# A two-layer diffusion trunk step on one core: four gate columns ahead of the feed-forward pairs, the residual affine on VectorE, two modulation vectors moved

## The chip, the core and the metric

One core of a Trainium2 chip. Its engines run unsynchronized instruction queues: TensorE (PE, matmuls and transposes, with its weight loads listed as PEld), VectorE (DVE), ScalarE (ACT), GpSimd (POOL) and SyncE (SP), which here only issues DMAs. The metric is the device time of one execution in microseconds (us); lower is better.

## What is computed

One inference step of a trunk of two post-norm layers over 512 latent tokens and 128 prompt tokens of width 1024. Each layer mixes the tokens (attention, a delta-rule scan and an HGRN scan), projects, normalizes, and runs a gated feed-forward block. Cut to what the change touches:

```python
def trunk_layer(x, mod, ...):
    shift_m, scale_m, gate_m, shift_f, scale_f, gate_f = jnp.split(mod.astype(x.dtype), 6, axis=-1)
    z = (x * (1 + scale_m) + shift_m) @ w_in
    o, k_c, v_c, s_d, s_h = token_mixers(z, ...)
    x = layer_norm(ALPHA * x + gate_m * (o @ w_out), ln_g[0], ln_b[0])
    gt, up = jnp.split((x * (1 + scale_f) + shift_f) @ w_ffn_in, 2, axis=-1)
    x = layer_norm(ALPHA * x + gate_f * ((jax.nn.silu(gt) * up) @ w_ffn_out), ln_g[1], ln_b[1])
    return x, k_c, v_c, s_d, s_h
# per layer l: mod_p = silu(c_ctx) @ w_mod[l] + b_mod[l], mod_s = silu(c) @ w_mod[l] + b_mod[l]
```

The matrices are float32: w_in 1024 x 3856, w_out 1024 x 1024, w_ffn_in 1024 x 5632 (gate columns, then up columns), w_ffn_out 2816 x 1024, w_mod 1024 x 6144.

## The kernel before

Tokens are five tiles of 128 (four latent, one prompt). A float32 product is made of three matmuls on a high and a low part of both factors: the high part of a weight is a cast on ACT, the low part a subtraction on DVE, both into an `hl` tile (four buffers); the weight itself first lands in a `raw` tile of 512 KB (three buffers, loaded from SP's queue). The code lists the work in program order; a planner orders each engine's instructions by its own estimate of what is ready, and `behind()` keeps the instructions under it after those in `AFTER`, engine by engine.

**Output projection and entry.** `pss` holds five PSUM tiles for columns 0 to 511; the loop takes one weight unit (`rowunit`, two of eight row blocks) after another over all five token tiles, and then `residual` runs for the five tiles: multiply by the gate, `r = ALPHA * x + ...`, statistics, all DVE. Columns 512 to 1023 go tile by tile with the four units of `us1`, and behind each tile `ln_next` normalizes and modulates it and `ffn_T` transposes it into `xT` (transposes named pta). `ffn_sums`, called at tiles 3 and 4, builds the sums and differences of token halves (`fS`, `fA`, `SX`) that the feed-forward product needs: per call eight DVE operations, two on POOL (named fa) and four casts on ACT. `ln_rest` then gives `r` its normalization and affine (one ACT, two POOL operations per tile, the POOL ones `r<-r,lg` and `r<-r,lb`); `r` is needed when part 0 of the output products adds to it.

**Pairs.** The input product of the block runs as one level of a seven-product scheme (Strassen-Winograd) over 22 column blocks f. Column f has a gate half and an up half, each 1024 x 128. `pair_a(f)` takes two of the seven products (pfa, 24 matmuls) with the gate columns `gts[f]`; `pair_b(f)` the other five (pfc, pfb, pfd, 60 matmuls) with sums of gate and up weights: two preparations on POOL (`t<-raw`, `raw<-raw`), two on DVE, three `in_two` (cast and subtraction). `gate_unit(f)` loads both halves and converts the gate half. Pairs stand in the order a0, a1, b0, b1, a2, b2, a3, and so on. After each part of `FF_PARTS` (four pairs in the first) come the output products pfo, 120 matmuls of 512 columns for four pairs; part 0 adds to `r` on DVE, later parts on POOL. The gate rows of the block (modulation vector 5) are loaded into the tiles `lg` and `lb_` once these are free.

**Modulation.** Vectors 3, 4, 2 and 5 of a layer's six are made in `mods()` during its own mixer, turn by turn with attention and HGRN (`run`, `TURNS`): eight loads of w_mod into `raw` and 32 small matmuls (psm) each. Vectors 0 and 1 of layer 1 are made by `modulation_wide` between the pairs of layer 0: loads from POOL's queue, multiply-adds on DVE (`mw`), 32 matmuls in all.

Of the kernel before, what the change touches and what calls it, by code (L numbers as in the profile page):

```python
# [10 lines left out]
F32 = mybir.dt.float32  # L11
# [26 lines left out]
C_AQ, C_AK, C_AV, C_BQKV, C_BG, C_CQ, C_CF, C_CI = 0, 512, 1024, 1536, 2304, 2576, 2832, 3344  # L38
NB = 272
FF_PARTS = ((0, 4), (4, 8), (8, 12), (12, 16), (16, 18), (18, 22))  # L40

# [66 lines left out]
def tile_trunk(  # L108
# [64 lines left out]
    def tt(eng, out, a, b, op):  # L173
        return eng.tensor_tensor(out, a, b, op)  # L174
# [68 lines left out]

    AFFINE = [[((G, G),), ((G, G),)], ((V, V), (G, G),)]

# [236 lines left out]

    def modulation_wide(l, vecs, pool):


        for i in vecs:
            dst = modrow[l][:, i * D:(i + 1) * D].rearrange("j (g n) -> j g n", g=4)
            for j in range(2):
                S.dma_start(bm[QR[j]], b_mod[l][i * D:(i + 1) * D].rearrange("(g n) -> g n", g=4))
            ms = cp.tile([P, 256], F32, tag="ms", name=f"ms{l}_{i}")  # L490
            for hf in range(2):
                w8 = pool.tile([P, 2, 1024], F32, tag="hb", bufs=1, name=f"mw{l}_{i}_{hf}")
                acc, raw2 = (w8[:, x].rearrange("p (j n) -> p j n", j=2) for x in range(2))
                for k in range(KT):
                    raw = raw2[:, k % 2]
                    G.dma_start(raw, w_mod[l][k * P:(k + 1) * P, i * D + 512 * hf:i * D + 512 * hf + 512])
                    for j in range(2):
                        ck = cm[:, k, j:j + 1]
                        if k == 0:
                            A.activation(acc[:, j], raw, AF.Copy, scale=ck)  # L500
                        else:
                            V.scalar_tensor_tensor(acc[:, j], raw, ck, acc[:, j], ALU.mult, ALU.add)
                    if k % 2:
                        yield
                ps = psS("m", f"psm{l}_{i}_{hf}")
                hs = slice(64 * hf, 64 * hf + 64)
                for g in range(2):
                    for j in range(2):
                        mm(ps[64 * hf + 32 * g:64 * hf + 32 * g + 32, :256], onesj[:, j],
                           acc[:, j, g * 256:(g + 1) * 256], start=(j == 0), stop=(j == 1))  # L510
                tt(V, ms[hs], ps[hs, :256], bm[hs], ALU.add)
            for j in range(2):
                S.dma_start(dst[j], ms[QR[j]])

    def rowload(pool, src, tag, t=None):
# [59 lines left out]


    def ln_rest(r, mv, rs, g, b, dst):
        eng = AFFINE[0][CUR[0]] if dst is None else AFFINE[1]
        V.scalar_tensor_tensor(rs[:, :, 1], mv[:, :, 0], -1.0, rs[:, :, 0], ALU.mult, ALU.mult)
        for tau in range(NT):  # L580
            A.activation(r[tau], r[tau], AF.Identity, scale=rs[:, tau, 0:1], bias=rs[:, tau, 1:2])
            em, ea = eng[tau % len(eng)]
            tt(em, r[tau], r[tau], g, ALU.mult)
            tt(ea, r[tau], r[tau], b, ALU.add)
            if dst is not None:
                S.dma_start(dst[tau * P:(tau + 1) * P, :], r[tau])

# [783 lines left out]
    for l in range(DEPTH):  # L1371
# [41 lines left out]
        def mods():  # L1413
            yield from modulation(l, (3, 4, 2, 5))
            yield
            affine(l, 4, 3, (l, 0), praw, "raw", 3)
            yield

        held = {}
# [135 lines left out]
        pss = [psS("n", f"pop{l}_0_{tau}") for tau in range(NT)]  # L1555
        for n_, i in enumerate((2, 3, 0, 1)):
            u = rowunit(w_out[l], 2 * i, 2, 0, 512)
            for tau in range(NT):
                gemm_N(pss[tau], 512, xT, tau, [(u, [2 * i, 2 * i + 1])], first=(n_ == 0), last=(n_ == 3))
        us1 = [(rowunit(w_out[l], 2 * i, 2, 512, 512), [2 * i, 2 * i + 1]) for i in (2, 3, 0, 1)]  # L1560
        for tau in range(NT):
            residual(pss[tau], gm[tau >= LT][:, :512], r[tau], r[tau], 0, st[tau])

        def load_pair(f):
            g_, u_ = (raw_unit(Wi[:, c0 + f * P:c0 + f * P + P].rearrange("(k p) n -> p k n", p=P), KT, P)[0]
                      for c0 in (0, DFF))
            return g_, u_

# [11 lines left out]
        def gate_unit(f):  # L1580
            raws[f] = load_pair(f)
            gts[f] = in_two(raws[f][0], 1024, hl_tile())

        gate_unit(0)
        for tau in range(NT):
# [18 lines left out]

        def mods_wide():
            yield from modulation_wide(l + 1, range(2), fp)
            affine(l + 1, 1, 0, (l, 1), praw, "raw", 3)

        wide = mods_wide() if l + 1 < DEPTH else iter(())


# [14 lines left out]
        def pair_a(f):  # L1626
            if f not in gts:
                gate_unit(f)
            gt_ = gts.pop(f)
            a_ = psS("g", f"pfa{l}_{f}")  # L1630
            prod(a_, gt_, 0, "11")
            s1 = fp.tile([P, HT], F32, tag="s1", bufs=2, name=f"s1_{l}_{f}")
            A.copy(s1, a_[:, :HT])  # L1633
            prod(a_, gt_, 4, "12", start=False)
            sg = fp.tile([P, NTOK], F32, tag="sg", bufs=2, name=f"sg{l}_{f}")
# [44 lines left out]

        pair_a(0)
        pair_a(1)
        for part, (f0, f1) in enumerate(FF_PARTS):
            nk = f1 - f0
            last = part == len(FF_PARTS) - 1
            for f in range(f0, f1):
                pair_b(f, f - f0)
                if 1 <= f < NFF - 1:
                    pair_a(f + 1)
                for _ in range(2):  # L1690
                    next(wide, 0)
            if part == 0:
                gf = [rowload(None, modvec(l, 5, j), None, t_) for j, t_ in enumerate((lg, lb_))]
            if last:
                for _ in wide:
                    pass
# [90 lines left out]
```

## Time and profile before

| what | value |
|---|---|
| median of three runs | 2152.37 us (2149.19 to 2155.8) |
| the profiled execution | 2161.62 us |
| its span, first to last instruction | 2159.5 us |
| mean granted clock of PE, as a share of full | 0.934 |
| busy: PE, DVE, POOL, ACT | 1926.4, 1494.9, 963.1, 809.4 us |

The span holds the start (to 41 us), layer 0's projections and mixer (to 543), its output projection and entry (to 662), its feed-forward block (to 1110), and the same for layer 1 (mixer to about 1593, pair 0 at 1717, end 2160). Stage times below are microseconds from the span's start. A wait in square brackets is idle time of an engine just before the instruction, with what ended it.

### The profile page before, as it was taken

The numbers are of one execution on the slowest core, as the hardware profiler recorded it, in microseconds if no ns is written. First come the engines' busy times: TensorE is split into PE (matmuls) and PEld (weight loads), VectorE is DVE, ScalarE is ACT, GpSimd is POOL, SyncE is SP. The second block draws the span as 40 slices with busy tenths as digits, with TensorE's granted clock in tenths as the row PEclk, the third lists the DMA queues.
The fourth block names the chain that finished last, engine by engine and source line by source line (L and its number), as shares of the span: only waits on it lengthen the run. The fifth ranks groups of instructions, "written<-read, shape, count | busy, mean of one in ns | idle before, by whom it ended". The sixth has DMA issues, their size and how long they took to land. (4 is left out here: it accounts for less than half of the span.)

```text
span 2159.5 us, 37748 instructions
## 1 busy us (share of the span) xinstructions
PE 1926.4 (89%) x14818; PEld 1698.0 (79%) x14818; DVE 1494.9 (69%) x2556; ACT 809.4 (37%) x1582; POOL 963.1 (45%) x1040
## 2 busy tenths in 40 slices
PE   7999997778946999999989999978899399999996
PEld 5988986557736888998979988865677399899995
DVE  5458525767598897676776794358867978666676
ACT  3532312547242333343325423226742343334331
POOL 0374334755173224324354843358642712432444
PEclk8999997887977999999999999989999699999998
DMA  9323226771503433232244232277631132222222
GB/s 298 105 73 123 89 73 161 218 214 41 185 30 94 150 108 88 80 91 76 86 136 137 84 119 86 82 182 230 201 142 54 47 100 72 85 88 89 78 70 77
DMA packets 235334, 245.15 MB, mean 114 GB/s; under 512 B 19498, under 2 KB 182294, under 8 KB 235158
## 3 DMA queue, kind: packets, MB, share of 16 engines
q1 hardware_dynamic: 210422, 214.69, 32.1%
q10 hardware_dynamic: 22176, 19.67, 3.5%
q0 software_dynamic: 2560, 8.39, 1.2%
q8 instruction: 117, 1.92, 0.4%
q14 instruction: 59, 0.48, 0.1%
HBM read 214.52 MB, written 28.18 MB: 112 GB/s over the span
## 5 line engine op out<-in xcount | busy, mean ns | idle before, releaser
L174 DVE TENSOR_TENSOR hl<-raw,hl 128x1024 fp32r<-128x1024 f32 (+1 forms) x210 | 281.1, 1342 | 92.6 <-ACT hl L271 77.3
L171 PE MATMUL pfo<-hl,ha 128*128 128x512 f32 x1320 | 313.4, 395 | 1.1 <-DVE ft L174 0.6
L171 PEld LDWEIGHTS pfo<-hl,ha 128*128 128x128 f32 x1320 | 246.0, 188 | 60.8 <-DVE ft L174 1.3
L174 POOL TENSOR_TENSOR r<-r,ft 128x512 f32<-128x512 f32 x96 | 143.8, 1519 | 250.1 <-DVE ft L174 249.5
L171 PE MATMUL pfc<-sx,hl 128*128 128x320 f32 x1056 | 176.0, 315 | 58.8 <-ACT hl L1571 54.1
L171 PEld LDWEIGHTS pfc<-sx,hl 128*128 128x128 f32 x1056 | 163.1, 192 | 63.7 <-ACT hl L1571 56.3
L171 PE MATMUL pfa<-xT,hl 128*128 128x320 f32 x1056 | 181.7, 321 | 20.5 <-ACT s L1633 10.9
L171 PEld LDWEIGHTS pfa<-xT,hl 128*128 128x128 f32 x1056 | 167.1, 198 | 24.8 <-ACT s L1633 12.2
L174 POOL TENSOR_TENSOR t<-raw 128x512 f32<-128x512 f32 x44 | 64.4, 1463 | 265.2 <-DMA raw<-in_w_ffn_in_dram 119.7
L271 ACT CAST hl<-raw 128x1024 fp32r<-128x1024 f32 (+2 forms) x122 | 125.4, 1035 | 134.1 <-DMA raw<-in_w_ffn_out_dram 44.5
L1571 ACT CAST hl<-raw 128x1024 fp32r<-128x1024 f32 x88 | 92.3, 1051 | 209.9 <-PE pfo L171 96.9
L171 PE MATMUL paq<-xT,hl 128*128 128x320 f32 x768 | 123.2, 317 | 0.6 <-ACT az L1264 0.6
L171 PEld LDWEIGHTS paq<-xT,hl 128*128 128x128 f32 x768 | 115.7, 190 | 3.4 <-issue 1.2
L171 PE MATMUL pop<-hl,xT 128*128 128x512 f32 x480 | 113.3, 395 | 1.1 <-ACT ae_p L1157 1.1
L174 POOL TENSOR_TENSOR hK<-hK,hT 64x256 f32<-64x256 f32 x120 | 90.3, 753 | 42.7 <-PE ph L171 36.6
L171 PEld LDWEIGHTS pop<-hl,xT 128*128 128x128 f32 x480 | 89.1, 188 | 20.8 <-ACT ae_p L1157 1.2
L174 DVE TENSOR_TENSOR ft<-pfo,lg 128x512 f32<-128x512 f32 x96 | 64.2, 683 | 54.8 <-PE pfo L171 48.1
L174 DVE TENSOR_TENSOR t<-raw,t 128x512 f32<-128x512 f32 x88 | 74.4, 845 | 35.3 <-POOL t L174 35.1
L171 PE MATMUL pbq<-xT,hl 128*128 128x320 f32 x576 | 90.1, 314 | 1.0 <-DVE hl L174 0.4
L171 PE MATMUL pfd<-xT,hl 128*128 128x320 f32 x528 | 87.0, 314 | 4.1 <-DVE ft L174 3.4
L171 PE MATMUL pfb<-sx,hl 128*128 128x320 f32 x528 | 89.4, 314 | 0.0
L171 PEld LDWEIGHTS pbq<-xT,hl 128*128 128x128 f32 x576 | 86.0, 190 | 2.6 <-issue 0.8
(404 smaller groups left out, 4371.3 us busy)
## 6 DMA issues: line engine op xcount, KB each, us to landing
raw<-in_w_ffn_in_dram SPq DMA_DIRECT2D x88, 512.0 KB
raw<-in_w_mod_dram SPq DMA_DIRECT2D x64, 512.0 KB
raw<-in_w_in_dram SPq DMA_DIRECT2D x56, 512.0 KB
raw<-in_w_ffn_out_dram SPq DMA_DIRECT2D x44, 512.0 KB
pc<-in_w_mod_dram SPq DMA_DIRECT2D x8, 1024.0 KB
raw<-in_w_out_dram SPq DMA_DIRECT2D x16, 512.0 KB
mw<-in_w_mod_dram POOLq DMA_DIRECT2D x32, 256.0 KB, 3.1
qksc<-az SPq DMA_DIRECT2D x16, 320.0 KB
```

The lines of the kernel that those rows point to most:

```text
L171: nc.tensor.matmul(out, lhsT, rhs, start=start, stop=stop, **kw)
L174: return eng.tensor_tensor(out, a, b, op)
L271: A.copy(hl[:, 0, :kt * n], raw[:, :kt * n])
L1571: A.copy(tile_[:, 0, :n], raw)
```

## The change

- `gate_unit(f)` loads only the gate half for f below `AHEAD` = 4; `pair_b` loads both halves then. `pair_a(0)` to `pair_a(3)` stand ahead of the first `pair_b`; the intermediate results of columns 2 and 3 lie in a new tile `xtra`.
- `ln_rest` is dropped from the entry. `ln_tile` does the same for one tile with two `scalar_tensor_tensor` operations on DVE, called behind pairs 0, 1, 2 (tiles 0 to 2) and 3 (tiles 3 and 4). `ln_rest` stays for the end of layer 0.
- `modulation_wide` is removed; vectors 0 and 1 of layer 1 are made in layer 0's `mods()`, after the other four.
- The first half of the output projection loads all four units first, runs two of them over all tiles, then the other two tile by tile with `residual` behind each tile.

```diff
+AHEAD = 4
...
-    AFFINE = [[((G, G),), ((G, G),)], ((V, V), (G, G),)]
+    AFFINE = ((V, V), (G, G))
...
-    def modulation_wide(l, vecs, pool):
...
+    def ln_tile(r, mv, rs, g, b, tau):
+        V.scalar_tensor_tensor(r[tau], r[tau], mv[:, tau, 0:1], g, ALU.subtract, ALU.mult)
+        V.scalar_tensor_tensor(r[tau], r[tau], rs[:, tau, 0:1], b, ALU.mult, ALU.add)
...
             affine(l, 4, 3, (l, 0), praw, "raw", 3)
             yield
+            if l + 1 < DEPTH:
+                yield from modulation(l + 1, (0, 1))
+                affine(l + 1, 1, 0, (l, 1), praw, "raw", 3)
+                yield
...
-        for n_, i in enumerate((2, 3, 0, 1)):
-            u = rowunit(w_out[l], 2 * i, 2, 0, 512)
-            for tau in range(NT):
-                gemm_N(pss[tau], 512, xT, tau, [(u, [2 * i, 2 * i + 1])], first=(n_ == 0), last=(n_ == 3))
+        us0 = [(rowunit(w_out[l], 2 * i, 2, 0, 512), [2 * i, 2 * i + 1]) for i in (2, 3, 0, 1)]
+        for tau in range(NT):
+            gemm_N(pss[tau], 512, xT, tau, us0[:2], last=False)
+        for tau in range(NT):
+            gemm_N(pss[tau], 512, xT, tau, us0[2:], first=False)
+            residual(pss[tau], gm[tau >= LT][:, :512], r[tau], r[tau], 0, st[tau])
         us1 = [(rowunit(w_out[l], 2 * i, 2, 512, 512), [2 * i, 2 * i + 1]) for i in (2, 3, 0, 1)]
-        for tau in range(NT):
-            residual(pss[tau], gm[tau >= LT][:, :512], r[tau], r[tau], 0, st[tau])
...
         def gate_unit(f):
-            raws[f] = load_pair(f)
-            gts[f] = in_two(raws[f][0], 1024, hl_tile())
+            g_ = load_col(0, f)
+            if f >= AHEAD:
+                raws[f] = (g_, load_col(DFF, f))
+            gts[f] = in_two(g_, 1024, hl_tile())
...
-        with behind():
-            ln_rest(r, mv, rs, lg, lb_, None)
...
-            g_, u_ = raws.pop(f)
+            g_, u_ = raws.pop(f) if f in raws else (load_col(0, f), load_col(DFF, f))
...
-        pair_a(0)
-        pair_a(1)
+        xtra = fp.tile([P, 2048], F32, tag="hb", bufs=1, name=f"xtra{l}")
+        for f in range(AHEAD):
+            pair_a(f)
...
                 pair_b(f, f - f0)
-                if 1 <= f < NFF - 1:
+                if AHEAD - 1 <= f < NFF - 1:
                     pair_a(f + 1)
-                for _ in range(2):
-                    next(wide, 0)
+                if part == 0:
+                    for tau in range(f, NT if f == f1 - 1 else f + 1):
+                        ln_tile(r, mv, rs, lg, lb_, tau)
```

## Rows read from the trace of the kernel before

**Rows 1.** The page, busy us, share of the span and instructions of each engine.
```profile
PE 1926.4 (89%) x14818; PEld 1698.0 (79%) x14818; DVE 1494.9 (69%) x2556; ACT 809.4 (37%) x1582; POOL 963.1 (45%) x1040
```

**Rows 2.** Stretches: length, busy us of five engines, PE's clock, DMA share, GB/s.
```profile
608.00:662.20 54.20, 14.63 (x66) 12.90 (x65) 51.98 (x37) 20.06 (x27) 41.55 (x23) 0.63 0.11 35
662.20:751.40 89.20, 83.79 (x448) 73.27 (x448) 76.67 (x110) 30.15 (x45) 24.94 (x28) 0.94 0.45 139
751.40:842.20 90.80, 84.85 (x473) 75.83 (x474) 77.40 (x111) 28.63 (x42) 29.38 (x26) 0.94 0.31 94
...
1663.00:1716.60 53.60, 16.67 (x73) 14.13 (x73) 51.35 (x37) 19.38 (x28) 42.23 (x17) 0.66 0.03 10
1716.60:1794.00 77.40, 76.85 (x434) 70.33 (x435) 59.21 (x87) 27.41 (x40) 16.34 (x10) 0.97 0.34 102
1794.00:1871.30 77.30, 77.30 (x458) 71.81 (x458) 52.08 (x76) 27.18 (x41) 25.90 (x17) 1.00 0.27 82
```

**Rows 3.** Timeline of PE, entry of layer 1: start, length, instruction, wait before it.
```profile
1664.76 0.64 PE L171 MATMUL pfa<-xT,hl 128*128 128x320 f32 x1 [0.74 <-ACT xT L1517]
...
1686.44 3.29 PE L171 MATMUL pfa<-xT,hl 128*128 128x320 f32 x12 [3.28 <-ACT s L1633]
1716.58 0.90 PE L171 MATMUL pfc<-sx,hl 128*128 128x320 f32 x2 [26.84 <-ACT hl L1571]
```

**Rows 4.** Groups of DVE, 1663 to 1717: busy us, mean ns | idle before.
```profile
L174 DVE TENSOR_TENSOR fs<-fs,xT 128x512 f32<-128x512 f32 x3 | 8.4, 2803 | 0.0
L174 DVE TENSOR_TENSOR sx<-fs,sx 128x768 fp32r<-128x768 f32 x3 | 6.9, 2299 | 1.0 <-ACT sx L1532 1.0
L174 DVE TENSOR_TENSOR sx<-fs,sx 128x512 fp32r<-128x512 f32 x3 | 6.4, 2120 | 0.0
L174 DVE TENSOR_TENSOR fs<-fs,xT 128x768 f32<-128x768 f32 x3 | 5.0, 1658 | 0.0
L174 DVE TENSOR_TENSOR xT<-fa,xT 128x768 fp32r<-128x768 f32 x1 | 3.1, 3094 | 0.0
```

**Rows 5.** Timeline of DVE, both entries, the two shapes while POOL is idle.
```profile
1676.92 0.95 DVE L174 TENSOR_TENSOR fs<-fs,xT 128x768 f32<-128x768 f32 x1
...
650.96 0.68 DVE L174 TENSOR_TENSOR fs<-xT,fs 128x512 f32<-128x512 f32 x1
```

**Rows 6.** Groups of POOL, 1663 to 1717.
```profile
L174 POOL TENSOR_TENSOR r<-r,lg 128x1024 f32<-128x1024 f32 x5 | 15.3, 3067 | 0.0
L174 POOL TENSOR_TENSOR r<-r,lb 128x1024 f32<-128x1024 f32 x5 | 14.4, 2890 | 0.0
```

**Rows 7.** Stretch of layer 1 from pair 0 to the output products, 1717 to 1769.
```profile
sum 52.00, PE 51.45 PEld 49.85 DVE 39.38 ACT 21.10 POOL 12.50; mean PE 25.72 PEld 24.92 DVE 19.69 ACT 10.55 POOL 6.25
```

**Rows 8.** Groups of DVE, 1663 to 1717: a scalar_tensor_tensor of 128x1024.
```profile
L572 DVE SCALAR_TENSOR_TENSOR xma<-r,mv,sc 128x1024 f32<-128x1024 f32 x1 | 1.3, 1274 | 0.0
```

**Rows 9.** Timeline of POOL, part 0 of layer 1, one pair's preparation.
```profile
1752.25 1.30 POOL L174 TENSOR_TENSOR t<-raw 128x512 f32<-128x512 f32 x1 [9.55 <-DMA raw<-in_w_ffn_in_dram]
```

**Rows 10.** Groups of DVE, 662 to 842 (parts 0 and 1 of layer 0).
```profile
L502 DVE SCALAR_TENSOR_TENSOR mw<-mw,cm 128x512 f32<-128x512 f32 x50 | 39.5, 825 | 5.0 <-DMA mw<-in_w_mod_dram 2.7 <-ACT mw L500 2.3
```

**Rows 11.** Stretch of layer 0's mixer behind its last modulation vector, 480 to 543.
```profile
sum 63.00, PE 51.18 PEld 45.88 DVE 50.31 ACT 42.27 POOL 37.47; mean PE 17.06 PEld 15.29 DVE 16.77 ACT 14.09 POOL 12.49
```

**Rows 12.** Timeline of PE in the mixer: eight modulation matmuls.
```profile
462.42 0.64 PE L171 MATMUL psm<-raw,cm 128*32 128x256 f32 x8
```

**Rows 13.** Waits of PE, 385 to 480: us in total, times, longest.
```profile
PE psm L171 <- DMA raw<-in_w_mod_dram: 8.9, 9, 2.7
```

**Rows 14.** SP's queue: the first and last w_mod loads shown, 29 in all.
```profile
394.80 13.93 SPq L252 DMA_DIRECT2D raw<-in_w_mod_dram  x8
...
463.34 8.06 SPq L252 DMA_DIRECT2D raw<-in_w_mod_dram  x5
```

**Rows 15.** Timeline of PE, output projection of layer 0: its first and its last matmuls.
```profile
543.40 5.86 PE L171 MATMUL pop<-hl,xT 128*128 128x512 f32 x24 [1.06 <-ACT ae_p L1157]
...
560.62 36.65 PE L171 MATMUL pop<-hl,xT 128*128 128x512 f32 x156
```

More of the change, by code (lines that the diff above doesn't have):

```diff
@@ L481, in modulation @@
             yield
-    def modulation_wide(l, vecs, pool):
[L486 to L513, printed above, removed]
     def rowload(pool, src, tag, t=None):
@@ L574, in ln_next @@
         return into(xm, tau, f"pt{name}") if into else to_T(xm, xT, tau, f"pt{name}")
+    def ln_tile(r, mv, rs, g, b, tau):
+        V.scalar_tensor_tensor(r[tau], r[tau], mv[:, tau, 0:1], g, ALU.subtract, ALU.mult)
+        V.scalar_tensor_tensor(r[tau], r[tau], rs[:, tau, 0:1], b, ALU.mult, ALU.add)
     def ln_rest(r, mv, rs, g, b, dst):
-        eng = AFFINE[0][CUR[0]] if dst is None else AFFINE[1]
+        eng = AFFINE
         V.scalar_tensor_tensor(rs[:, :, 1], mv[:, :, 0], -1.0, rs[:, :, 0], ALU.mult, ALU.mult)
@@ L584, in ln_rest @@
             tt(ea, r[tau], r[tau], b, ALU.add)
-            if dst is not None:
-                S.dma_start(dst[tau * P:(tau + 1) * P, :], r[tau])
+            S.dma_start(dst[tau * P:(tau + 1) * P, :], r[tau])
     def ln_last(r, st, mv, rs, g, b, tau, dst):
@@ L1555, in tile_trunk, with load_col @@
         pss = [psS("n", f"pop{l}_0_{tau}") for tau in range(NT)]
-        for n_, i in enumerate((2, 3, 0, 1)):
-            u = rowunit(w_out[l], 2 * i, 2, 0, 512)
-            for tau in range(NT):
-                gemm_N(pss[tau], 512, xT, tau, [(u, [2 * i, 2 * i + 1])], first=(n_ == 0), last=(n_ == 3))
-        us1 = [(rowunit(w_out[l], 2 * i, 2, 512, 512), [2 * i, 2 * i + 1]) for i in (2, 3, 0, 1)]
-        for tau in range(NT):
-            residual(pss[tau], gm[tau >= LT][:, :512], r[tau], r[tau], 0, st[tau])
[L1564 to L1567, printed above, removed]
+        us0 = [(rowunit(w_out[l], 2 * i, 2, 0, 512), [2 * i, 2 * i + 1]) for i in (2, 3, 0, 1)]
[4 more added lines that the diff above has]
+            residual(pss[tau], gm[tau >= LT][:, :512], r[tau], r[tau], 0, st[tau])
+        us1 = [(rowunit(w_out[l], 2 * i, 2, 512, 512), [2 * i, 2 * i + 1]) for i in (2, 3, 0, 1)]
+        def load_col(c0, f):
+            return raw_unit(Wi[:, c0 + f * P:c0 + f * P + P].rearrange("(k p) n -> p k n", p=P), KT, P)[0]
         def in_two(raw, n, tile_):
@@ L1603, in tile_trunk @@
         sc_, sp = pool(f"V{l}", "left")
[L1605 to L1609, printed above, removed]
         XQ = {"11": lambda xi, k: xT[:, xi, k, :HT], "12": lambda xi, k: xT[:, xi, 4 + k, :HT],
@@ L1631, in pair_a @@
             prod(a_, gt_, 0, "11")
-            s1 = fp.tile([P, HT], F32, tag="s1", bufs=2, name=f"s1_{l}_{f}")
+            if 2 <= f < AHEAD:
+                s1, sg = xtra[:, (f - 2) * 960:(f - 2) * 960 + HT], xtra[:, (f - 2) * 960 + HT:(f - 1) * 960]
+            else:
+                s1 = fp.tile([P, HT], F32, tag="s1", bufs=2, name=f"s1_{l}_{f}")
+                sg = fp.tile([P, NTOK], F32, tag="sg", bufs=2, name=f"sg{l}_{f}")
             A.copy(s1, a_[:, :HT])
             prod(a_, gt_, 4, "12", start=False)
-            sg = fp.tile([P, NTOK], F32, tag="sg", bufs=2, name=f"sg{l}_{f}")
             A.activation(sg[:, :HT], a_[:, :HT], AF.Silu)
@@ L1694, in tile_trunk @@
             if last:
-                for _ in wide:
-                    pass
                 close(sc_)
```

## The prediction

> **What bounds the kernel now.** TensorE (PE) is busy 1926 of 2159.5 us [rows 1], so only the stretches in which it waits can give time. I read four views in this order: the page's busy line, the table of stretches over both feed-forward blocks, the timeline of PE in the entry, and the groups of VectorE (DVE) and GpSimd (POOL) there. The stretches are cut where the timeline of PE shows the first gate matmul, the first matmul of pair 0, and the last output matmul of a part.
>
> Two things stand out in the table [rows 2]. First, the entry: in layer 0 PE works 14.6 of 54.2 us, in layer 1 16.7 of 53.6, at a granted clock of 0.63 and 0.66 of full, while DVE works 52.0 and 51.4 of them. The longest wait is 26.84 us ahead of pair 0 of layer 1 [rows 3], after two gate columns are done; what it waits for hangs on DVE's chain of sums. Second, parts 0 and 1 last 89.2 and 90.8 us in layer 0, but 77.4 and 77.3 in layer 1, which runs the same products; only layer 0 carries the wide modulation.
>
> **Part 1, the wide modulation leaves layer 0's pairs.** The price is read off directly: 89.2 - 77.4 = 11.8 and 90.8 - 77.3 = 13.5, together 25.3 us. The cause fits: DVE spends 39.5 us of those two parts in 50 multiply-adds that layer 1 doesn't have [rows 10]. Its DMAs on POOL's queue and its 32 small matmuls go too and are inside the same difference. The entry of layer 0 is also longer: 54.2 us [rows 2] against 1716.58 - 1664.76 = 51.8 in layer 1 [rows 3], 2.4 us, from the multiply-adds that begin there. Term: -27.7, to within 2.
>
> **Part 2, the ten residual operations leave POOL in the entry.** ffn_sums needs 16 DVE operations per layer, eight of 768 columns and eight of 512. In layer 1 they took 8.4 + 6.9 + 6.4 + 5.0, and four single ones of 2.8 to 3.1 (11.8 together), 38.5 us [rows 4]. Beside an idle POOL the same shapes take 0.95 and 0.68 [rows 5], 8 x 0.95 + 8 x 0.68 = 13.0. So 25.5 us of the chain is DVE held up by POOL, whose r operations last 2.9 to 3.1 us each and fill the time [rows 6]. After the change these ten are gone. What stays are four fa operations; by the 0.95 and 0.68 rows a DVE operation is held up by about its neighbour's length, which I put at 1.3 each, 5.2 us. Two more gate columns add two low-part subtractions of 128x1024, 1.27 each by the nearest row [rows 8], 2.5 us. That leaves 25.5 - 5.2 - 2.5 = 17.8, and with 1.2 for gaps between DVE and ScalarE (ACT) in the chain pair 0 starts 16.6 us earlier, at 1700 on the old scale.
>
> The Trainium skill (SBUF — State Buffer, SBUF: two separate sides) says that DVE and POOL share one port pair as an exclusive lock, taken by a DVE operation with two SBUF inputs, and that the loser waits for the whole instruction. The trace agrees in the entry (3.09 us against 0.95). By the same rule the change's own ten DVE operations, which have two SBUF inputs, would hold POOL's pair preparation up; the first rival below is that case.
>
> **Part 3, four gate columns first.** Two more columns of 24 matmuls go into the gap. At the low clock 12 took 3.29 us [rows 3], so 48 take 13.2; at full clock a part of four pairs has 336 matmuls of 320 columns and 120 of 512, 168,960 columns in 77.3 us [rows 2], so one of 320 takes 0.146 and 48 take 7.0. Of the 26.8 us about 10 are left after part 2, and the columns fill them: no cost, and PE has 7 us less to do in part 0. Their price is four more loads of 512 KB per layer, since the gate column is fetched again for pairs 0 to 3. A load takes 2.64 us at the pace of the modulation loads (29 in the 76.6 us from 394.8 to 471.4 [rows 14]). Pair 0 to 3 then turn in a ring of three raw buffers: load 2.64, two POOL operations of 1.30 [rows 9], a cast and a subtraction at 1.27 each [rows 8], 7.8 us per pair, below what DVE takes (next). Hidden; if it weren't, 2.64 per pair.
>
> **Part 4, the residual affine on DVE in part 0.** Ten scalar_tensor_tensor of 128x1024 at 1.27 us [rows 8] are 12.7 us per layer. In the 52 us from pair 0 to the output products DVE is busy 39.4 and PE 51.5 [rows 7]. After: 39.4 - 2.5 + 12.7 = 49.6 for DVE, 51.5 - 7.0 = 44.5 for PE. So DVE becomes the bound of these pairs, and the 7 us that part 3 saves PE are not booked: part 0 stays near 52 us. I take off 1.6 for waits at 96% of an engine, so 16.6 - 1.6 = 15 us per layer. The gate rows can now be loaded only after the last of the ten; two loads (5.3 us) hide behind output products that wait in PSUM banks, else that is their cost. Lower end: POOL's eight preparations of part 0 each lose 1.3 to the ten, 10.4 us, and 15 becomes 5. Upper end: PE's waits of 26.8 and 3.3 [rows 3] go whole less about 2, 28. Term: 2 x -15 = -30, from -56 to -10.
>
> **Part 5, two modulation vectors move into layer 0's mixer.** Each is 8 loads and 32 small matmuls, in groups of 8 taking 0.64 us [rows 12]: 64 matmuls are 5.1 us of PE. PE's queue is in order, and what stands behind a vector's matmul is attention: in the stretch with four vectors PE waited 8.9 us for w_mod loads [rows 13], 2.2 per vector, 4.5 for two. So 9.6 if all is on the path. Cover: from the end of the present vectors to the output projection are 63 us with PE busy 51.2 [rows 11], and DMA moves little there; 16 loads at 2.64 last 42 us, which leaves about 20 for the output weights, whose loads stand behind them on SP's queue. I take 9; low end 3 (PE's 11.8 idle us take the matmuls in), high end 18 (the stalls twice and the output weights 4 us late).
>
> **Part 6, the projection by tile.** PE runs its last 156 matmuls in one piece of 36.65 us [rows 15]; there is no wait that an earlier residual could remove, so no gain. The second half's weights need the first half's buffers, now freed only at its end: two casts and a subtraction at 1.27 each [rows 8] are 3.8 us, against 18 matmuls x 0.235 = 4.2 of cover. 0, at most 2 per layer.
>
> **The sum.** -27.7 - 30 + 9 + 0 = -48.7. The profiled execution took 2161.6 us, its span 2159.5; that gives 2112.9 there. The median of the runs is 2152.4, 9 us below that execution; taken from it, 2103.7, so 2104.
>
> **The rivals.** (a) DVE and POOL hold each other up in part 0, so that the entry's gain is given back there: 5 per layer, -27.7 - 10 + 9 = -28.7, 2124. For: DVE would be at 96%; against: DVE's idle 12.6 us of 52 [rows 7] lie where POOL waits for loads (9.55 us before one preparation [rows 9]), and the ten operations depend on nothing there. (b) PE's waits go whole, since the planner spreads the ten operations into idle spots and the output products: 28 per layer, -74.7, 2078. Against: DVE's sum above. (c) Slower: the modulation becomes the bound of layer 0's mixer. Place: attention's last head, behind w_mod matmuls in PE's queue. Price: all 16 loads on the path (42.2), then five output weight loads (13.2), then the affine rows, which keep one of three buffers for some 10 us: 65.4 against gains of 57.7, 2160. It decides from 57.7 on. For: PE did wait at 9 of these loads [rows 13]; against: never over 2.7 us. (d) The change doesn't do what it says: the planner orders each engine by its own estimate, columns 2 and 3 come after pair 0, and the projection loses 2 per layer: about 8 per layer for the entry, -27.7 - 16 + 9 + 4 = -30.7, 2122.
>
> **Chances.** My forecast 0.62, (a) 0.16, (b) 0.12, (c) 0.05, (d) 0.05. The range 2075 to 2132 holds (a), (b) and (d) with the bounds of the modulation's price around (a) and leaves out (c) and the tails. A measurement tells about 0.3%, 6.5 us, from no change. Faster: 0.91; same: 0.04, where (a) meets the modulation's high end; slower: 0.05.
>
> **What would show it.** In the profile after: parts 0 and 1 of layer 0 near layer 1's; no r operations on POOL in the entry, the 16 sums at 0.7 to 1.8 us each, the wait before pair 0 below 5 us, and PE's clock there above 0.66; DVE above 90% from pair 0 to the output products; the stretch from the first refill of w_mod [rows 14] to the first output-projection matmul of layer 0 [rows 15], now 543.4 - 394.8 = 148.6 us, 3 to 18 longer. I am wrong in part 4 if part 0 shrinks well below 77 us after pair 0 starts, and in part 5 if that stretch grows by more.

## The result and the profile after

| what | before | after |
|---|---|---|
| median | 2154.1 us (2149.2 to 2160.4) | 2119.4 us (2117.0 to 2120.6) |
| ratio to before, 95% interval | | 0.9836 [0.9808, 0.9864] |
| the profiled execution, its span | 2161.6, 2159.5 us | 2120.6, 2118.8 us |

The kernel became 1.6% faster, 34.7 us by the medians. The forecast was 2104 with a range of 2075 to 2132: sign and range hold, the point is 15.4 us too low.

The page of the changed kernel, busy us of each engine, answers [rows 1]: PE does the same work, DVE has lost 52 us (the wide multiply-adds above all), POOL 65 (above all the ten residual operations of each layer, 29.7 us in layer 1's entry by [rows 6]).

```profile
PE 1922.7 (91%) x14914; PEld 1690.1 (80%) x14914; DVE 1442.9 (68%) x2516; ACT 795.1 (38%) x1564; POOL 897.9 (42%) x988
```

The same stretches as [rows 2] in the changed kernel: entry, part 0 and part 1 of layer 0, then of layer 1; length, busy us of PE, PEld, DVE, ACT and POOL, PE's granted clock, DMA share, GB/s.

```profile
623.80:660.60 36.80, 21.84 (x114) 19.87 (x112) 34.74 (x37) 16.73 (x27) 16.80 (x8) 0.78 0.25 72
660.60:732.10 71.50, 70.04 (x386) 63.13 (x387) 56.97 (x85) 24.08 (x34) 15.87 (x10) 0.97 0.34 104
732.10:809.30 77.20, 77.20 (x458) 71.71 (x457) 52.03 (x76) 27.18 (x40) 26.01 (x17) 1.00 0.27 82
1646.40:1682.00 35.60, 23.30 (x114) 21.80 (x112) 33.53 (x36) 16.73 (x27) 16.71 (x7) 0.69 0.26 75
1682.00:1754.10 72.10, 70.25 (x386) 62.76 (x387) 58.65 (x85) 23.89 (x34) 15.48 (x10) 0.98 0.34 102
1754.10:1831.40 77.30, 77.30 (x459) 71.79 (x458) 52.09 (x76) 27.19 (x40) 25.87 (x17) 1.00 0.28 82
```

The entries are 17.2 and 16.2 us shorter, PE's clock in them (a mean between its two levels, 1.2 and 2.4 GHz, which are 0.5 and 1.0) is up from 0.63 and 0.66 to 0.78 and 0.69, and layer 0's parts 0 and 1 now last what layer 1's do. Cut by the same events on PE's timeline, both spans come apart like this (us; the mixer from the first w_mod matmul to the first projection matmul, the tail from the last projection matmul to the first gate matmul, the entry from there to pair 0):

| stage | before, layer 0, 1 | after, layer 0, 1 | difference |
|---|---|---|---|
| start to the first w_mod matmul of layer 0 | 394.1 | 391.2 | -2.9 |
| mixer of layer 0 | 149.3 | 159.3 | +10.0 |
| output projection | 58.0, 56.4 | 59.5, 59.2 | +4.3 |
| tail | 6.6, 4.5 | 13.8, 14.2 | +16.9 |
| entry | 54.1, 51.8 | 36.9, 35.6 | -33.4 |
| part 0 | 89.2, 77.4 | 71.5, 72.1 | -23.0 |
| part 1 of layer 0 | 90.8 | 77.2 | -13.6 |
| layer 1's projections and mixer | 493.4 | 495.4 | +2.0 |
| all the rest | | | -1.0 |
| span | 2159.5 | 2118.8 | -40.7 |

One large line of it stood in no term of the sum: the tail, +16.9. The timeline of PE at the end of layer 1's projection in the changed kernel (start, length, instruction, wait before it) shows PE standing before the transposes (`pta`, two groups of four per tile) of the third tile. It waits for that tile's normalized and modulated rows, `xma`:

```profile
1633.13 0.63 PE L1489 MATMUL pta<-c_ident,xma 128*128 128x128 f32 x4 [0.54 <-DVE xT L176]
1643.42 1.11 PE L1489 MATMUL pta<-c_ident,xma 128*128 128x128 f32 x4 [9.65 <-POOL xma L176]
1645.62 1.11 PE L1489 MATMUL pta<-c_ident,xma 128*128 128x128 f32 x4 [1.09 <-POOL xma L176]
1646.38 0.61 PE L173 MATMUL pfa<-xT,hl 128*128 128x320 f32 x1
```

And the timeline of DVE before that, same kernel and columns. L548 and L549 are the two operations of `ln_tile`:

```profile
1618.64 1.23 DVE L176 TENSOR_TENSOR xma<-xma,sc 128x1024 f32<-128x1024 f32 x1 [0.18 <-ACT xma L536]
1619.79 1.28 DVE L548 SCALAR_TENSOR_TENSOR r<-r,mv,lg 128x1024 f32<-128x1024 f32 x1
1620.98 2.32 DVE L176 TENSOR_TENSOR xma<-xma,sc 128x1024 f32<-128x1024 f32 x1
1623.22 2.30 DVE L548 SCALAR_TENSOR_TENSOR r<-r,mv,lg 128x1024 f32<-128x1024 f32 x1
1625.45 0.68 DVE L176 TENSOR_TENSOR rt<-pop,gm 128x512 f32<-128x512 f32 x1
1626.05 3.95 DVE L549 SCALAR_TENSOR_TENSOR r<-r,rs,lb 128x1024 f32<-128x1024 f32 x2
1629.92 0.68 DVE L1478 SCALAR_TENSOR_TENSOR r<-r,rt 128x512 f32<-128x512 f32 x1
...
1640.97 1.27 DVE L548 SCALAR_TENSOR_TENSOR r<-r,mv,lg 128x1024 f32<-128x1024 f32 x1
1642.16 2.28 DVE L543 SCALAR_TENSOR_TENSOR xma<-xma,rs,sh 128x1024 f32<-128x1024 f32 x1
1644.37 2.28 DVE L548 SCALAR_TENSOR_TENSOR r<-r,mv,lg 128x1024 f32<-128x1024 f32 x1
```

The code lists the ten residual operations behind pairs 0 to 3. In the built kernel the planner has put all ten before pair 0, because nothing holds them: a tile's operations are ready once its statistics are. Four of them, 7.5 us, stand before the residual and statistics of the later tiles, and each later step of the chain to `xma`, the transposes and the gate columns is as much later. POOL's part of that chain runs at the same time:

```profile
1620.00 8.91 POOL L176 TENSOR_TENSOR xma<-xma,sh 128x512 f32<-128x512 f32 x4 [1.74 <-issue]
```

DVE operations that take 1.27 us alone take 2.0 to 2.3 beside it. (In layer 0 the same wait for `xma` is shorter, 5.7 us at its longest.)

### The profile page after: what moved, and what is told of

It reads as the page before. It is cut to its first block, busy times and chain, and to the rows that moved or that the text cites. A ratio compares the mean times of both kernels' runs of the same rounds, so it can differ in the third digit from the quotient of the medians.

```text
span 2118.8 us, 37807 instructions
## 1 busy us (share of the span) xinstructions
PE 1922.7 (91%) x14914; PEld 1690.1 (80%) x14914; DVE 1442.9 (68%) x2516; ACT 795.1 (38%) x1564; POOL 897.9 (42%) x988
## 3 DMA queue, kind: packets, MB, share of 16 engines
q1 hardware_dynamic: 221046, 227.27, 34.7%
## 5 line engine op out<-in xcount | busy, mean ns | idle before, releaser
L176 POOL TENSOR_TENSOR t<-raw 128x512 f32<-128x512 f32 x44 | 71.0, 1614 | 317.7 <-DMA raw<-in_w_ffn_in_dram 148.9
L173 PEld LDWEIGHTS pfc<-sx,hl 128*128 128x128 f32 x1056 | 161.1, 190 | 18.6 <-ACT hl L1547 13.8
L173 PE MATMUL pop<-hl,xT 128*128 128x512 f32 x480 | 115.8, 401 | 1.7 <-ACT hl L273 1.7
```

Of the source, the lines that this page charges most:

```text
L173: nc.tensor.matmul(out, lhsT, rhs, start=start, stop=stop, **kw)
```

## Experiments

The theory under test is the reading above: the ten operations, drawn forward, made the tail. Its rivals are that the projection by tile made it, and, for the entry, that the gain came from something other than POOL being free. Times are medians with the range of the executions; ratios are to the kernel before, with the 95% interval; stages are cut as in the table and read from one execution of each kernel. The kernel before was timed again beside each group of experiments, with medians of 2157.1 us (1 to 4), 2158.7 (5 to 8) and 2156.1 (9 to 11) where the result has 2154.1: a difference of medians between two groups is uncertain by some 3 to 5 us.

**1. The operations held behind their pair.** Each tile's `ln_tile` may only follow the last DVE operation of its own pair; nothing else is changed.

```diff
-            out(1, u4)
+            return out(1, u4)
...
-                pair_b(f, f - f0)
+                done = pair_b(f, f - f0)
...
-                        ln_tile(r, mv, rs, lg, lb_, tau)
+                        with tc.issue_after(done.ins):
+                            ln_tile(r, mv, rs, lg, lb_, tau)
```

> Each tile's two residual operations are kept behind the last VectorE operation of their own pair, as the listing of the code has them. Theory H (in the changed kernel the planner drew the ten operations forward into the chain of ln_next, and that is what made the stretch from the last projection matmul to the first gate matmul 13.8 and 14.2 us instead of 6.6 and 4.5): that stretch is back at 5 to 7 us in both layers, pair 0 follows the first gate matmul after 35 to 37 us as in the changed kernel, and the time falls by 6 us if VectorE is then the bound of part 0 (77 us there), by up to 17 if it isn't (72). Rival P (the tile-wise first half of the projection made that stretch longer): it stays at 13 to 14 us and the time within 3 us of the changed kernel's 2119.

Measured: 2102.2 us (2097.1 to 2104.5), ratio 0.974 [0.9724, 0.9756], 17 us faster than the change. Tail 7.3 and 6.9, entry 32.6 and 32.0 (35 to 37 was expected), part 0 75.9 and 77.0. The time fell by the most that was expected, though part 0 is as long as in the case that gave it 6 us. The waits of PE from the end of layer 1's projection to pair 0 (us in total, times, longest), first in the changed kernel, 1600 to 1683, then in this one, 1600 to 1654:

```profile
PE pta L1489 <- POOL xma L176: 10.7, 2, 9.7
PE pfc L173 <- ACT hl L1547: 6.4, 1, 6.4
PE pta L1489 <- DVE xT L176: 3.0, 2, 2.5
```

```profile
PE pfc L173 <- ACT hl L1547: 6.9, 1, 6.9
PE pta L1489 <- DVE xT L176: 4.1, 1, 4.1
PE pfa L173 <- DVE hl L176: 2.4, 1, 2.4
```

The wait for `xma` is gone, and nothing as long takes its place. Tail, entry and part 0 together went from 122.2 and 121.9 to 115.8 and 115.9, that is 12.4 us for both layers. The spans differ by more, 23.5 (this profiled execution lay 5 us below its median): a shorter projection has 3.9 of the rest, and 6.0 lie ahead of the first projection matmul of layer 0 (544.4 against 550.5), where the code is the same; I put no cause to that part (see the last section). So 12.4 of the 17 us are in the stages that the edit touches, and the tails have 13.8 of their 16.9 back; the 3.1 that stay have no cause shown.

**2. The output projection as before, the rest as changed.** The rival for the tail was the projection by tile itself.

```diff
-        us0 = [(rowunit(w_out[l], 2 * i, 2, 0, 512), [2 * i, 2 * i + 1]) for i in (2, 3, 0, 1)]
-        for tau in range(NT):
-            gemm_N(pss[tau], 512, xT, tau, us0[:2], last=False)
+        for n_, i in enumerate((2, 3, 0, 1)):
+            u = rowunit(w_out[l], 2 * i, 2, 0, 512)
+            for tau in range(NT):
+                gemm_N(pss[tau], 512, xT, tau, [(u, [2 * i, 2 * i + 1])], first=(n_ == 0), last=(n_ == 3))
```

> The changed kernel with the first half of the output projection unit by unit again, residuals behind it. Theory H: the stretch from the last projection matmul to the first gate matmul stays at 13 to 15 us; only the projection itself, 1.5 and 2.9 us longer in the changed kernel, gives back 0 to 4 us. Rival P: the stretch falls to 5 to 7 us and the time by about 17.

Measured: 2115.8, 2117.6 and 2117.7 us, ratio 0.9812 [0.9796, 0.9829]. The profiled execution was disturbed (8691 us), so its stage times say nothing. The order of DVE's instructions can be read in it: all ten operations stand ahead of pair 0 in both layers, four of them before the residuals of the later tiles, as in the changed kernel. Had the projection by tile made the tail, 17 us would have come back; 1.8 did by the medians, 5 by the ratios. Experiment 1, which keeps the projection by tile, has the short tail.

**3. The ten operations left out.** The normalization and affine of the residual are missing from the output.

```diff
-                if part == 0:
-                    for tau in range(f, NT if f == f1 - 1 else f + 1):
-                        ln_tile(r, mv, rs, lg, lb_, tau)
```

> The ten residual operations of each layer are left out altogether, so the residual enters part 0 without its normalization and affine. It is the floor of what they cost wherever they stand. Theory H: stretch before the first gate matmul 5 to 7 us, part 0 at 70 to 72, time lower by 17 to 22 us. Rival P: the stretch stays at 13 to 14, and only VectorE's 12.7 us per layer go, off the path: lower by 0 to 5.

Measured: 2107.2 us (2106.2 to 2111.6), ratio 0.9765 [0.9749, 0.9781]. Tail 7.3 and 9.2, entry 31.5 and 33.4, part 0 72.1 and 71.1; together 110.9 and 113.7. So the ten operations cost 11.3 and 8.2 us per layer where the planner had put them, and 4.9 and 2.2 where experiment 1 holds them. Part 0 without them lasts what it lasts in the changed kernel (71.5, 72.1): there they are indeed not in part 0. The time fell by 12 us and not by the 17 to 22 expected. That the whole run is nevertheless slower than experiment 1's, with less work, is the matter of experiments 9 to 11: layer 1's projections and mixer lasted 502.1 us here and 494.0 there.

**4. The operations held behind the sums of the entry** instead of behind pairs.

```diff
-                ffn_sums(*((0, 4 * P - HT) if tau == 3 else (4 * P - HT, HT)))
+                summed = ffn_sums(*((0, 4 * P - HT) if tau == 3 else (4 * P - HT, HT)))
...
+                        with tc.issue_after(summed.ins):
+                            ln_tile(r, mv, rs, lg, lb_, tau)
```

> The ten operations are kept only behind the last low part of ffn_sums, so the planner may place them anywhere in part 0. Theory H: stretch before the first gate matmul 5 to 7 us; against the kernel with the operations tied to their pairs this shows what their place in part 0 is worth: 0 if VectorE's sum decides, up to 6 us slower if they now stand ahead of pair 0's preparation. Rival P: 13 to 14 us there, time unchanged.

Measured: 2125.3 us (2124.9 to 2130.0), ratio 0.9855 [0.9841, 0.987]. DVE's timeline in layer 1 before pair 0 (which starts at 1681):

```profile
1671.62 6.06 DVE L548 SCALAR_TENSOR_TENSOR r<-r,mv,lg 128x1024 f32<-128x1024 f32 x5
1677.60 1.28 DVE L549 SCALAR_TENSOR_TENSOR r<-r,rs,lb 128x1024 f32<-128x1024 f32 x1
1678.80 0.68 DVE L176 TENSOR_TENSOR t<-raw,t 128x512 f32<-128x512 f32 x1
1679.40 3.67 DVE L549 SCALAR_TENSOR_TENSOR r<-r,rs,lb 128x1024 f32<-128x1024 f32 x3
```

The tail is short (7.3, 7.0), but DVE's preparation of pair 0 now stands behind six of the operations, and PE waits 13.9 us before pair 0 where it waited 6.9 in experiment 1:

```profile
PE pfc L173 <- ACT hl L1547: 13.9, 1, 13.9
```

The entry is 39.9 and 39.0. The same ten operations of 1.2 us each cost 8 to 13 us per layer against experiment 3's sums (124.3 and 123.7 here) wherever they stand ahead of pair 0, be it before the transposes or behind the sums. Against experiment 1 the time is 23 us higher where up to 6 was expected: of the 27.8 us between the two spans, 16.3 are tail, entry and part 0, and 11.4 layer 1's projections and mixer (experiments 9 to 11).

**5. The residual operations on ACT and POOL as before, with four columns first.** This takes back the move of the operations (parts 2 and 4 of the prediction) and keeps the rest.

```diff
+        with behind():
+            ln_rest(r, mv, rs, lg, lb_, None)
...
-                if part == 0:
-                    for tau in range(f, NT if f == f1 - 1 else f + 1):
-                        ln_tile(r, mv, rs, lg, lb_, tau)
```

> The changed kernel with the residual normalization and affine where the kernel before had it: five ScalarE and ten GpSimd operations per layer, behind the last transposes; four gate columns first as changed. Theory C (GpSimd's operations hold VectorE's sums up; that is what made pair 0 late): pair 0 follows the first gate matmul after 49 to 54 us as before the change, though four gate columns stand ahead of it, part 0 is 66 to 72 us, and the sum of the three stretches (last projection matmul to first gate matmul, to pair 0, part 0) is 122 to 132 us per layer against 116 with the operations tied to their pairs. Rival: the wait for pair 0 came from the gate columns and their buffers; then pair 0 follows after 32 to 38 us here too and the sum is near 110.

Measured: 2133.5 us (2129.7 to 2138.5), ratio 0.9884 [0.9861, 0.9907]. Entry 52.6 and 53.4, part 0 72.7 and 73.2. DVE's groups in the entry of layer 1 (busy us, mean ns; `fs`, `sx` and `fa` are the tiles of the sums, fS, SX and fA), first this kernel, then experiment 1, whose POOL has no residual operations:

```profile
L176 DVE TENSOR_TENSOR fs<-fs,xT 128x768 f32<-128x768 f32 x3 | 7.2, 2389 | 0.0
L176 DVE TENSOR_TENSOR fs<-fs,xT 128x512 f32<-128x512 f32 x3 | 6.2, 2067 | 0.1
L176 DVE TENSOR_TENSOR sx<-fs,sx 128x512 fp32r<-128x512 f32 x3 | 5.3, 1759 | 0.0
```

```profile
L176 DVE TENSOR_TENSOR fs<-fs,xT 128x768 f32<-128x768 f32 x3 | 3.3, 1101 | 0.0
L176 DVE TENSOR_TENSOR fs<-fs,xT 128x512 f32<-128x512 f32 x3 | 3.1, 1046 | 0.0
L176 DVE TENSOR_TENSOR sx<-fs,sx 128x512 fp32r<-128x512 f32 x3 | 2.1, 684 | 0.7 <-ACT sx L1510 0.7
```

The sums, which read two tiles in SBUF, take twice as long and more beside POOL's `r` operations. With four columns but the operations on POOL the entry stays where it was before. So the gain of the entry is the operations' leaving POOL, and none of it the columns': tail, entry and part 0 of layer 1 sum to 133.5 here and 133.8 before. Against experiment 1 the sums (132.6 and 133.5; 115.8 and 115.9) are 16.7 and 17.6 us longer; the prediction had 15, its 16.6 less 1.6 given back in part 0. Part 0 and the sums lie just above what was expected (72 and 132).

What a DVE operation reads makes a difference here. In the same entry, before the `r` operations begin, two additions of POOL run beside one DVE operation with both inputs in SBUF (`sx`) and one that reads the transposes from PSUM (`pta`):

```profile
1649.69 1.81 POOL L176 TENSOR_TENSOR fa<-xT,fa 128x768 f32<-128x768 f32 x1 [4.75 <-ACT fa L1492]
1651.58 2.44 POOL L176 TENSOR_TENSOR fa<-fa,xT 128x768 f32<-128x768 f32 x1
```

```profile
1650.46 1.86 DVE L176 TENSOR_TENSOR sx<-fs,sx 128x768 fp32r<-128x768 f32 x1 [0.90 <-ACT sx L1511]
1652.24 0.68 DVE L176 TENSOR_TENSOR xT<-pta,xT 128x512 fp32r<-128x512 f32 x1
```

With POOL idle the first shape takes 0.95 us (experiment 1, at 1648.88) and the second 0.69 (here, at 1648.28).

The Trainium skill (SBUF — State Buffer, SBUF: two separate sides) describes an exclusive lock on a port pair between POOL and a DVE operation with two SBUF inputs. The trace agrees: beside POOL 1.86 against 0.95 us for two SBUF inputs, 0.68 against 0.69 with one input in PSUM.

**6. The wide modulation back, on top of experiment 1.** Vectors 0 and 1 leave layer 0's mixer and are made by `modulation_wide` between the pairs again, from pair 4 on.

```diff
-            if l + 1 < DEPTH:
-                yield from modulation(l + 1, (0, 1))
-                affine(l + 1, 1, 0, (l, 1), praw, "raw", 3)
-                yield
...
+                for _ in range(2 if f >= 4 else 0):
+                    next(wide, 0)
```

> The kernel with the operations tied to their pairs, but modulation vectors 0 and 1 of layer 1 made wide on VectorE between the pairs of layer 0 again, from pair 4 on (parts 1 and 2), since the buffer is taken before that. Theory W (the wide modulation costs VectorE-bound pairs 25 us, the vectors in the mixer 7 to 10): parts 1 and 2 of layer 0 are 12 to 14 us longer each, the stretch from the first modulation matmul to the projection of layer 0 7 to 10 us shorter, the time 14 to 20 us higher than 2102. Rival: the wide modulation only cost where VectorE was full for another reason; then parts 1 and 2 grow by under 5 each and the time is the same or lower.

Measured: 2111.1 us (2106.6 to 2116.1), ratio 0.978 [0.9757, 0.9802]. The mixer is 145.7 us, 7.0 shorter than in experiment 1. Parts 0 to 2 of layer 0 (columns as in [rows 2]):

```profile
635.10:715.80 80.70, 72.80 (x386) 65.31 (x387) 72.76 (x95) 25.39 (x37) 18.28 (x17) 0.94 0.41 125
715.80:804.70 88.90, 84.59 (x482) 74.25 (x481) 84.65 (x119) 30.84 (x47) 31.55 (x34) 0.98 0.44 136
804.70:889.00 84.30, 81.61 (x465) 73.92 (x464) 68.27 (x96) 27.24 (x40) 36.79 (x26) 0.98 0.28 83
```

They sum to 253.9 against 230.4 in experiment 1 (75.9 + 77.3 + 77.2): 23.5 us for the wide form, where the prediction read 25.3 off the table before. The 23.5 are 4.8 in part 0, where the first multiply-adds already run (at 699 us), 11.6 in part 1 and 7.1 in part 2; 12 to 14 in each of the last two was expected. DVE is busy 85 of 88.9 us in part 1. The time rose by 9 us and not by 14 to 20, less than 23.5 - 7.0, since layer 1's projections and mixer came out at 488.9.

**7. Two columns ahead instead of four, on top of experiment 1.**

```diff
-AHEAD = 4
+AHEAD = 2
...
-        xtra = fp.tile([P, 2048], F32, tag="hb", bufs=1, name=f"xtra{l}")
```

> The kernel with the operations tied to their pairs, but two gate columns first instead of four. Theory F (the columns only fill a wait of TensorE that stays anyway, and part 0 is held by VectorE): pair 0 0 to 3 us earlier after the first gate matmul, part 0 0 to 5 us longer, the sum of both within 3 us of 109 per layer, the time 0 to 6 us higher. Rival E (TensorE is the bound of part 0, so 48 matmuls moved ahead are worth 7 us per layer): sum 5 to 8 longer per layer, the time 10 to 16 us higher.

Measured: 2109.2 us (2104.1 to 2116.7), ratio 0.9773 [0.9746, 0.98]. Tail, entry and part 0: 114.3 and 113.1, 1.5 and 2.8 us less than with four columns. So columns 2 and 3 ahead of the pairs bring nothing, and 7 us of the time against experiment 1 are not from the entry: layer 1's projections and mixer lasted 506.8 against 494.0.

**8. The two vectors made between layer 0's pairs in the mixer's form** (loads, 32 small matmuls each), one step per pair from pair 4 on.

```diff
+        def mods_next():
+            yield from modulation(l + 1, (0, 1))
+            affine(l + 1, 1, 0, (l, 1), praw, "raw", 3)
...
+                if f >= 4:
+                    next(wide, 0)
```

> The kernel with the operations tied to their pairs, and the two vectors made with the small matmuls of the mixer's form, but one step per pair from pair 4 on in layer 0's feed-forward block. Theory M (in the mixer the price is the wait of TensorE's queue for w_mod loads, 8.9 us before and 9.5 now, more than the 5 us of matmuls): mixer of layer 0 7 to 10 us shorter, parts 1 to 3 of layer 0 together 5 to 8 us longer, the time 0 to 5 us lower. Rival: the sixteen loads of 512 KB take raw buffers from the pairs, parts 1 to 3 grow by 10 to 30 us and the time rises.

Measured: 2128.9 us (2126.0 to 2133.4), ratio 0.9865 [0.9841, 0.9889]. The mixer is 8.5 us shorter than in experiment 1, parts 0 to 2 last 77.3, 85.2 and 93.7, 25.8 longer together. So the rival was right and the theory, 5 to 8 us there and a time no higher, was not. Another 13.8 us are layer 1's projections and mixer (507.9). The mixer of layer 0 remains the cheapest of the three places.

**9 to 11. What moves layer 1's mixer.** Against experiment 1, experiments 3, 7 and 8 lost 8 to 14 us in a stage that no edit touched. PE's instructions from the end of layer 0 to the first projection matmul of layer 1 stand in the same order in the kernels of each line here (in the traces of experiments 1 and 5 but for a few neighbouring 64x64 matmuls), and in another order from line to line:

| kernels with one order of PE there | length of that stretch, us |
|---|---|
| before; experiment 6 | 493.4; 488.9 |
| experiments 1 and 5 | 494.0; 493.2 |
| the changed kernel; experiment 9 | 495.4; 496.9 |
| experiments 7 and 8 | 506.8; 507.9 |
| experiment 3 | 502.1 |
| experiment 4 | 505.5 |
| experiment 10 | 513.1 |
| experiment 11 | 509.2 |

Experiment 9 is experiment 1 with three columns ahead (`AHEAD = 3`), 10 is experiment 7 and 11 is experiment 1 with the operations held behind later pairs:

```diff
-                    for tau in range(f, NT if f == f1 - 1 else f + 1):
+                    for tau in ((), (0, 1), (2, 3), (4,))[f]:
```

```diff
-                    for tau in range(f, NT if f == f1 - 1 else f + 1):
+                    for tau in ((), (), (0, 1, 2), (3, 4))[f]:
```

> The tied kernel (e1_tied) with three gate columns ahead of the first pair instead of four. Between the end of layer 0 and the first projection matmul of layer 1 the code is unchanged; the built kernel lists PE's instructions there in the same order as the changed kernel does, and in another order than e1_tied and e7_ahead2. Theory 'order' (the length of that stretch goes by the order that the planner wrote, not by the number of columns): the stretch is 495.4, within 2, as in the changed kernel; the sum of projection tail, entry and part 0 lies between those of e1_tied (115.8, 115.9) and e7_ahead2 (114.3, 113.1), near 115 per layer; time 2102, within 4. Theory 'columns' (fewer columns ahead lengthen layer 1's mixer, 12.8 us for two of them): the stretch is 500, time 2107.

> e7_ahead2 (two columns ahead, residual operations tied) with the operations one pair later: tiles 0 and 1 behind pair 1, 2 and 3 behind pair 2, 4 behind pair 3. PE's order in layer 1's projections and mixer differs from that of every kernel so far. Theory 'order': the stretch from the end of layer 0 to the first projection matmul of layer 1 is another than e7_ahead2's 506.8 by more than 3 us, and the time is 2109.3 plus that difference, within 3. Theory 'columns' (two columns ahead make the stretch long): it stays at 507, within 2, time 2109. Tail, entry and part 0: 113.7 per layer, within 2, in both.

> e1_tied (four columns ahead) with the ten residual operations behind pairs 2 and 3 only (tiles 0 to 2 behind pair 2, 3 and 4 behind pair 3). PE's order in layer 1's projections and mixer is again a new one. Theory 'order': the stretch from the end of layer 0 to the first projection matmul of layer 1 is another than e1_tied's 494.0, and the time is 2102.2 plus that difference, within 3, since nothing waits for the operations before the output products of part 0. Theory 'load' (six operations of 1.27 us in one place hold up DVE's preparation of pair 3): part 0 is 3 to 6 us longer per layer than e1_tied's 75.9 and 77.0, time 2108 to 2114 with the stretch at 494.

Measured: experiment 9, 2102.8 us (2099.1 to 2103.7), ratio 0.9746 [0.9718, 0.9774], stretch 496.9, tail, entry and part 0 115.7 and 113.3. Experiment 10, 2114.2 us (2112.7 to 2117.5), 0.9804 [0.9776, 0.9832], stretch 513.1, tail, entry and part 0 115.5 and 114.1; by the order it should have been 2109.3 + 6.3 = 2115.6. Experiment 11, 2117.1 us (2115.4 to 2120.5), 0.9818 [0.9784, 0.9852], stretch 509.2; 2102.2 + 15.2 = 2117.4. Its part 0 is also longer, 79.4 and 79.6 against 75.9 and 77.0, as "load" had it in part. Tail, entry and part 0 together have 4.3 us more than in experiment 1, so that the time agrees within 0.3 us is luck: experiment 1's stages were read from an execution 5 us below its median.

So the theory "columns" falls (experiment 9 has the stretch of the changed kernel with four columns, whose order it shares) and "order" agrees with all three runs: after most edits of the entry the planner writes another order for the next layer's mixer, and the stretch then differs by up to 24 us (488.9 to 513.1). The order was never changed by itself, and kernels of one order differ by up to 4.5 us there (and by 6.6 in layer 0's mixer, see the last section), so for differences of that size it isn't shown. What in the order does it is only seen in its outcome. Layer 1's mixer in experiment 1, then in experiment 10 (columns as in [rows 2]):

```profile
1423.00:1557.70 134.70, 112.82 (x1296) 85.08 (x1295) 119.08 (x264) 89.93 (x271) 94.55 (x149) 0.96 0.53 168
```

```profile
1427.50:1577.80 150.30, 120.70 (x1305) 90.75 (x1304) 120.38 (x264) 90.59 (x270) 92.95 (x154) 0.90 0.49 151
```

Of 15.6 us, 7.7 are more idle time of PE and 7.9 are more busy time for nearly the same matmuls (1305 and 1296 records) at a granted clock of 0.90 instead of 0.96. Which of the reordered rows starts it stays open.

## Why the prediction was right, and where it was not

**Part 1, the wide modulation: right.** Part 1 of layer 0 lost 13.6 us (13.5 read off); of part 0's 17.7 us, 5.9 are more than the 11.8 read off, and layer 1, which never had the wide form, lost 5.3 there too. Experiment 6 has the price of the wide form a second way, 23.5 against 25.3.

**Part 2, POOL leaves the entry: right in mechanism and size.** Experiment 5 shows the mechanism, and 16.7 and 17.6 us per layer, net of part 0, for a predicted 15. In the changed kernel the entry lost 17.2 and 16.2, although four of the ten operations still stood in it. The wait before pair 0 was to be below 5 us and is 6.7 and 6.4. The two rows of [rows 5] don't lie beside an idle POOL (its operations start at 1676.93 and 651.12), but the lengths hold: in experiment 1 the same shapes take 0.94 and 0.68 us with POOL idle (at 1637.46 and 1649.75).

**Part 3, four columns first: right that they cost little.** The prediction left the 7 us that PE saves in part 0 unbooked, and rightly: experiments 7 and 9 show that, with the operations tied to their pairs, two or three columns do as well or up to 2.8 us better per layer.

**Part 4 is the step that failed.** It assumed that the ten operations would stand in part 0, where the code lists them, and priced them at the DVE sum of that part. They "depend on nothing there", as rival (a) says; the other half of that sentence I missed: an operation that nothing holds may be drawn forward. The planner did draw it, into the chain that ends at `xma`, and PE waited 9.65 us. That is 13.8 of the +16.9 in the tails, by experiment 1. The same placement gave part 0 back: not 1.6 us longer per layer but 5.3 to 5.9 shorter, which is the sign that the prediction had named for being wrong in part 4. Rival (d) had the planner ordering differently, but at the wrong place: the gate columns did come first; (b), the spreading of the operations, had it as a gain. Neither (a) nor (d) is what happened, though 2119.4 lies close to their 2124 and 2122.

With the operations in part 0 (experiment 1), the DVE sum itself was too high. One reason is the stretch. The 52 us of [rows 7] don't end where the output products begin: in the trace of before the first of them starts 44 us after pair 0:

```profile
1760.56 2.96 PE L171 MATMUL pfo<-hl,ha 128*128 128x512 f32 x12
```

So the ten operations had room among the output products too. The same 52 us from pair 0 of layer 1, in experiment 1:

```profile
sum 52.00, PE 48.40 PEld 46.33 DVE 44.84 ACT 18.18 POOL 12.72; mean PE 48.40 PEld 46.33 DVE 44.84 ACT 18.18 POOL 12.72
```

DVE is at 86%, not at 95% (49.6 of 52); in the changed kernel itself it is at 79%. Only six of the ten lie in it, which DVE's groups of the same stretch show; the other four ran later, among the output products:

```profile
L549 DVE SCALAR_TENSOR_TENSOR r<-r,rs,lb 128x1024 f32<-128x1024 f32 x3 | 4.9, 1627 | 0.0
L548 DVE SCALAR_TENSOR_TENSOR r<-r,mv,lg 128x1024 f32<-128x1024 f32 x3 | 4.9, 1622 | 0.0
```

Each takes 1.62 us, 0.35 more than the 1.27 priced: two of the six took 2.3 us, beside POOL's preparations. So rival (a)'s hold-up exists on DVE's side, but costs little. Part 0 is 75.9 and 77.0, against a predicted 79.0 (77.4 + 1.6).

**Part 5, the vectors in layer 0's mixer: right.** +10.0 for a predicted 9 (3 to 18). Over nine kernels with the two vectors the mixer lasts 153 to 159 us (mean 155.6), over three without them 144 to 149 (146.4): 9.2. PE's waits for w_mod there, changed kernel (us in total, times, longest), against 8.9 in [rows 13]:

```profile
PE psm L173 <- DMA raw<-in_w_mod_dram: 9.5, 10, 2.3
```

So the loads didn't become the bound, and rival (c) is out.

**Part 6, the projection by tile: 1.5 and 2.8 us per layer for a predicted 0 to 2.** By experiment 2 the old form of the projection brings 2 to 5 us in all. But in experiment 1 the form by tile lasts 57.9 and 56.9, within 0.5 us of before, so the loss in the changed kernel isn't shown to come from the form.

**The sum.** By spans the change brought 40.7 us and not 48.7. The 8.0 are the tail +16.9, the projection +4.3, the entries +2.2 (33.4 for 35.6), the mixer +1.0, and against them part 0 with -14.4 (23.0 for 8.6) and -2.0 in part 1 and the stages left out of the sum. A further 6.4 us are a matter of the base: the profiled execution before lay 7.5 us above its median of 2154.1, the one after 1.2 above its own, so the medians differ by 34.7 and the executions by 41.1 (0.3 more than the spans). I took differences of one execution off a median that lay below it. The last 1.7 are the median of before, 2152.4 then and 2154.1 with more runs; together these are, but for rounding, the 15.7 us from 2103.7, the forecast before it was rounded. That the result lies in the range is in part luck: the tail (+16.9), which no term held, and part 0 (-14.4) nearly cancel, and both come from the operations' standing elsewhere than assumed.

## What to carry to other kernels

Where a planner orders the instructions, moving an operation later in the code does not move it: ask what holds it there, and if nothing does, price it at the earliest place where its inputs are ready, above all on an engine whose chain others wait for. Here tying the operations to their pair gave 17 us, half as much again as the change itself (2102.2 against 2119.4, from 2154.1), and 12.4 of them in the stages that it touches. And compare such kernels stage by stage, not by their times: an edit in one stage can reorder a later one that it never touched, by more than the edit is worth.

## What the runs showed that was not expected

- A stage whose code is the same but ordered anew differed by up to 24 us (488.9 to 513.1). Between experiments 1 and 10 about half of the mixer's loss is PE running nearly the same matmuls at a lower granted clock (0.90 for 0.96), in a stretch in which it also waits more; that the waits lowered the clock isn't shown by itself.
- Layer 0's mixer with the two vectors varies from 152.7 to 159.3 us between kernels whose PE instructions up to the projection run in one and the same order in all nine traces. The cause isn't known. Differences of some 6 us between two of these kernels are therefore not put to an edit here, unless the stage shows it.
- Ten operations of 12.7 us in all cost 2 to 5 us per layer inside the pairs, 8 to 11 before the transposes and 10 to 13 behind the sums, where the wait before pair 0 is twice as long (13.9 for 6.9 us): the place, not the length, is the price.
